# Up 4 as a seven-product block, a new order of the wide pieces, and earlier rounding of their operands

## The chip, the cores and the metric

The kernel runs on 1 core of a Trainium2 chip. The metric is device microseconds of one execution. Three timed runs of the kernel before took 2169.24 to 2171.04 us, median 2170.62 us. Engines are named as in the profile: PE (TensorE matmul), PEld (its weight load), DVE (VectorE), ACT (ScalarE), POOL (GpSimd), SP (the queue that issues the DMAs).

## The reference, cut to what matters

Two decoder layers on 256 tokens of width 2048 in float32, each a mixer (attention) and a gated feed-forward block (FFN), each with a residual and a LayerNorm. The change is in the two FFN blocks alone:

```
D_MODEL = 2048; SEQ = 256; DEPTH = 2
D_FF = -(-8 * D_MODEL // (3 * 256)) * 256          # 5632

def swiglu(x, w_gate, w_up, w_down):
    return (jax.nn.silu(x @ w_gate) * (x @ w_up)) @ w_down

    for layer in range(DEPTH):
        ...                                         # y = mixer(x)
        x = layer_norm(DEEPNORM_ALPHA * x + y, ln_g[layer, 0], ln_b[layer, 0])
        y = swiglu(x, ffn_w_gate[layer], ffn_w_up[layer], ffn_w_down[layer])
        x = layer_norm(DEEPNORM_ALPHA * x + y, ln_g[layer, 1], ln_b[layer, 1])
```

## The kernel before, in words

**Pieces.** Every weight matrix is cut into chunks of 512 output columns, and a chunk into pieces of 256 rows by 512 columns (512 KB, one DMA on SP). FFN chunks are Gate f, Up f (f = 0 to 10, eight pieces each) and Down chunks (five groups of four; four or six pieces each). A float32 product is made of three fp32r products, so each piece is split after it has landed: ACT rounds it (`wh`), DVE subtracts to get the residue (`wl`), and PE multiplies three times (`mm3`, L116 to L119). A plain piece is 12 matmuls of 512 columns.

**Wide pieces** (`c.S`; here "seven-product pieces") use a Strassen-Winograd scheme over two token blocks, two row blocks and two column halves: seven products instead of eight, each in three fp32r matmuls, 21 matmuls of 256 columns (`emit_s`). They cost more beside PE: three DVE subtractions in the landed piece (`sraw`, L380 to L383), a rounding of 1792 columns on ACT (`sh`, L386) and a residue of 1792 columns on DVE (`sl`, L389), and at the end of a chunk a drain of four PSUM banks sA, sB, sC, sD (`drain_s`, one copy on ACT, five adds on DVE) in place of the plain chunk's direct use of its bank. Before the change Gate 2 to Gate 10 and Up 8 are made so, 80 pieces in a layer.

**Order of the work.** `ffn_part` writes a list of visits (one visit is one piece on PE). The plain chunks stand in a fixed order; the wide pieces (`gates`) are strewn among them at a rate: after plain visit k, as many wide pieces have been placed as the sum `want` says. `near` sets a minimum at some ends of Up chunks.

**After an Up chunk** the product silu(Gate f) x Up f lies in `gt` (DVE, L1085 for a plain Up, in two halves; L1089 for a seven-product Up), and `h_T` transposes it on PE (tile `tp`, one call for each half of the tokens), evacuates it to YH on ACT (L113) and YL on DVE (L114). `after_up` says behind which two visits the two calls stand. While wide pieces run, plain chunks and transposes share four PSUM banks in two pairs: a new plain chunk takes the pair that the one before did not use, and transposes go to the pair that the current plain chunk does not use (`ptile`, `sw`, `PAIRS`).

**Splits.** After every visit `feed_more` issues the DMAs and splits that find a free buffer: four for plain pieces, two for wide ones while these run. For a wide piece `feed_split` issues the DVE subtractions at once, and owes (`owe`) the rounding and the residue; `pay` issues them within a later split, when the debt is at least one split old. DVE and ACT run their instructions in the order in which they are issued, so that order is what each of them waits in.

Of the kernel before, what the change touches and what calls it, by code (L numbers as in the profile page):

```python
# [53 lines left out]
def trunk_kernel(ctx: ExitStack, tc: tile.TileContext, x, ab_w_in, b_f, ab_w_out,  # L54
# [67 lines left out]
    visits = []  # L122
    chunks = {}

    def add_chunk(name, xs, kslots, srcs, tags=None):
        subs = []
        o = 0
        for n in srcs[0]:
            subs.append((n, o))
            o += n  # L130
        c = Chunk(name, xs, kslots, subs, srcs[1], tags or ("mm",) * len(subs))
        c.n = o
        chunks[name] = c
        return c

    def kmajor(c, hs=None):
        for h in (range(c.nh) if hs is None else hs):
            visits.append((c, h, (0, 1)))
# [18 lines left out]
    def lead_begin(c):  # L157
        for t in (0, 1):
            for h in range(LEAD):
                visits.append((c, h, (t,)))  # L160
        kmajor(c, range(LEAD, c.nh))

    def rows(w, k0, cols):
        return [(o, n, w[k0:k0 + 256, c0:c0 + n].rearrange("(k p) c -> p k c", p=P))
                for o, n, c0 in cols]
# [31 lines left out]

    GROUPS = ((0, 1), (2, 3), (4, 5), (6, 7), (8, 9, 10))
    NF = 11
    UPS = (8,)  # L200
    PLAIN = (0, 1)
    h_done = set()
    after_up = {}
    win = {}

    def ffn_part(layer):
        def wide(nm, w, f):
            return add_chunk(f"{nm}{layer}_{f}", "X", K16, ([512], lambda h: rows(
                w[layer], h * 256, [(0, 512, f * 512)])))

        def down(gi):
            grp = GROUPS[gi]
            slots = [4 * (f % 4) + k for f in grp for k in range(4)]
            for n in range(4):
                c = add_chunk(f"d{layer}_{gi}_{n}", "Y", slots, (
                    [512], lambda h, n=n: rows(
                        w_down[layer], grp[0] * 512 + h * 256, [(0, 512, n * 512)])))
                if gi == len(GROUPS) - 1 and n == 3:
                    (lead_final if layer == 1 else lead_end)(c)
                else:  # L220
                    kmajor(c)

        g0 = wide("g", w_gate, 0)
        g0.pair = 0
        lead_begin(g0)
        base = len(visits)
        for f in range(NF):
            if f == 1:
                kmajor(wide("g", w_gate, 1))
            c = wide("u", w_up, f)  # L230
            if f in UPS:
                c.S = True
            else:
                kmajor(c)
            if f in (1, 3, 5, 7):
                down(f // 2)
        down(len(GROUPS) - 1)
        flat = visits[base:]
        del visits[base:]
        ends = {}  # L240
        for f in range(NF):
            if f not in UPS:
                e = ends[f] = max(k for k, v in enumerate(flat) if v[0].name == f"u{layer}_{f}")
                o = e + 2 - f % 2
                after_up[layer, f] = [(v[0].name, v[1], v[2]) for v in flat[o:o + 3]]
        gates = []
        for f in range(len(PLAIN), NF):
            c = wide("g", w_gate, f)
            c.S = True
            gates += [(c, h, (0, 1)) for h in range(8)]  # L250
            if f in UPS:
                gates += [(chunks[f"u{layer}_{f}"], h, (0, 1)) for h in range(8)]
        near = {ends[f] + 2 for f in (1, 3, 5, 7, 9)}
        ns, want = 0, 0.0
        for k, v in enumerate(flat):
            visits.append(v)
            want = max(want + (0 if k < 9 else 0.53 if k < 118 else 0.7),
                       ns + 1 if k in near else 0)
            while ns < min(len(gates), int(want)):
                visits.append(gates[ns])  # L260
                ns += 1
                c = gates[ns - 1][0]
                f = int(c.name[3:])
                if ns % 8 == 0 and c.name[0] == "g" and f not in UPS:
                    assert k < ends[f] - 1, (k, ns, ends)
        assert ns == len(gates)
        for f in UPS:
            e = max(k for k, v in enumerate(visits) if v[0].name == f"u{layer}_{f}")
            after_up[layer, f] = [(v[0].name, v[1], v[2]) for v in visits[e + 1:e + 3]]

    w_out_part("oa", ab_w_out[0])
    ffn_part(0)
    wi = mla_w_in[0]
    c = add_chunk("m0", "X", K16, ([512], lambda h: rows(wi, h * 256, [(0, 512, 0)])))
# [8 lines left out]
    for nm in order:  # L283
# [8 lines left out]
        kmajor(c)  # L292
    w_out_part("om", mla_w_out[0])
    ffn_part(1)


# [49 lines left out]
    def feed_dma(j, halves=False):  # L346
        if j >= len(pieces):
            return False
        c, h = pieces[j]
        got = take(raw_free, j)  # L350
        if got is None:
            return False
        rslot_of[j] = got
        r = got[1]
        v = r[:, :2 * c.n].rearrange("p (k c) -> p k c", k=2)
        for o, n, src in c.src(h):
            for k in ((slice(0, 1), slice(1, 2)) if halves else (slice(0, 2),)):
                nc.sync.dma_start(v[:, k, o:o + n], src[:, k, :])
        raws[j] = r
        return True  # L360

    whole = {}
    owed = []

    def pay(step):

        for o in list(owed):
            while o["fns"] and (step == "all" or o["age"] >= 1 and step == o["fns"][0][0]):
                o["fns"].pop(0)[1]()
            if not o["fns"]:  # L370
                owed.remove(o)

    def owe(key, act, dve, age=0):
        owed.append({"key": key, "age": age, "fns": [("act", act), ("dve", dve)]})

    def split_s(j):
        r = raws.pop(j)
# [16 lines left out]
    def feed_split(j, halves=False, part=None):  # L394
        if j >= len(pieces):
            return False
        c, h = pieces[j]
        n = 2 * c.n
        if part != 1:
            got = take(w_free, j) if j in raws else None  # L400
            if got is None:
                return False
            slot_of[j] = got
            if c.S:
                new = split_s(j)
                for o in owed:
                    o["age"] += 1
                pay("act")
                pay("dve")
                owe(j, *new)  # L410
                return True
            r = raws.pop(j)
            wh, wl = got[1]
            wts[j] = (wh[:, :n].rearrange("p (k c) -> p k c", k=2),
                      wl[:, :n].rearrange("p (k c) -> p k c", k=2))
            whole[j] = (r, wh, wl)
        r, wh, wl = whole[j]
        cuts = [(0, c.n), (c.n, n)] if halves or part is not None else [(0, n)]
        if part is not None:
            cuts = [cuts[part]]  # L420
        for a, b in cuts:
            nc.scalar.activation(wh[:, a:b], r[:, a:b], AF.Copy)  # L422
            pay("act")
            nc.vector.tensor_tensor(wl[:, a:b], r[:, a:b], wh[:, a:b].bitcast(F32),  # L424
                                    op=ALU.subtract)
            pay("dve")
        if part != 0:
            whole.pop(j)
            raw_free.append(rslot_of.pop(j))
        for o in owed:  # L430
            o["age"] += 1
        return True
# [3 lines left out]
    def fetch():  # L436
        while fs["nd"] < len(pieces) and feed_dma(fs["nd"]):
            fs["nd"] += 1

    def feed_more(lim):  # L440
        fetch()
        while fs["nsp"] < min(lim, len(pieces)) and feed_split(fs["nsp"]):
            fs["nsp"] += 1
            fetch()

    def mm_s(o, xt, w, j, q, first, last):
        h, l = xt
        nc.tensor.matmul(o, h, w[0][:, q], start=first, stop=False)  # L448
        nc.tensor.matmul(o, h, w[1][:, q], start=False, stop=False)  # L449
        nc.tensor.matmul(o, l, w[0][:, q], start=False, stop=last)  # L450
# [375 lines left out]
                        load_T(hd - 8)  # L826
        return done

    cur = [0]
    for g in range(4):  # L830
        chunks[f"v{g}"].done = v_evac(g, chunks[f"v{g}"])
        for u in range(2):
# [520 lines left out]
    for i, (c, h, toks, *half) in enumerate(visits):  # L1353
# [21 lines left out]
        if last_use[c.name, h] == i:  # L1375
            j = pid[c.name, h]
            if c.name == "v0" and h in (0, 2, 4):
                x_T(h + 2)
                feed_more(h + 3)
                x_T(h + 3)  # L1380
            w_free.append(slot_of.pop(j))
            feed_more(min(i + 3 if i <= 4 else 8 + 17 * (i - 4) // 10, hold.get((c.name, h, toks), 10 ** 6)))
# [75 lines left out]
```

## Time and profile before

| | |
|---|---|
| timed runs, median of 3 | 2170.62 us (2169.24 to 2171.04) |
| profiled execution, its own time | 2170.17 us |
| its span, first to last instruction | 2168.3 us |
| PE busy | 2131.5 us, 98% of the span |
| DVE busy | 1639.8 us, 76% |
| ACT busy | 1046.3 us, 48% |
| mean granted TensorE clock | 0.994 |

The span is the time from the first to the last instruction; 1.9 us of the execution lie outside it. PE is busy nearly all the time, so time is lost or won where PE waits, where its clock is low, and in how many columns it multiplies. A busy share of PE is made of modelled ends; the step from one matmul's start to the next one's is the safer measure.

### The profile page before, as it was taken

The numbers are of one execution on the slowest core, as the hardware profiler recorded it, in microseconds if no ns is written. First come the engines' busy times: TensorE is split into PE (matmuls) and PEld (weight loads), VectorE is DVE, ScalarE is ACT, GpSimd is POOL, SyncE is SP. The second block draws the span as 40 slices with busy tenths as digits, with TensorE's granted clock in tenths as the row PEclk, the third lists the DMA queues.
The fourth block names the chain that finished last, engine by engine and source line by source line (L and its number), as shares of the span: only waits on it lengthen the run. The fifth ranks groups of instructions, "written<-read, shape, count | busy, mean of one in ns | idle before, by whom it ended". The sixth has DMA issues, their size and how long they took to land.

```text
span 2168.3 us, 31334 instructions
## 1 busy us (share of the span) xinstructions
PE 2131.5 (98%) x12426; PEld 1865.3 (86%) x12426; DVE 1639.8 (76%) x2117; ACT 1046.3 (48%) x1210; POOL 94.5 (4%) x142
## 2 busy tenths in 40 slices
PE   9999999999999999989999999999999999999998
PEld 9899998788888888878878998878888888887886
DVE  5555656788888888888866676598887888888875
ACT  5444544455444454444534665355544444454451
POOL 2100000100000000000001330010000000000000
PEclk9999999999999999999999999999999999999999
DMA  8565556555565555555765544745654555555582
GB/s 287 170 206 165 172 185 216 192 184 190 169 208 191 194 194 189 183 184 173 258 214 163 176 133 143 274 139 182 204 195 165 187 198 189 198 166 173 200 282 78
DMA packets 230338, 410.39 MB, mean 189 GB/s; under 512 B 14088, under 2 KB 58160, under 8 KB 229168
## 3 DMA queue, kind: packets, MB, share of 16 engines
q1 hardware_dynamic: 230192, 408.40, 56.5%
q8 instruction: 97, 1.59, 0.3%
q14 instruction: 49, 0.40, 0.1%
HBM read 402.56 MB, written 5.78 MB: 188 GB/s over the span
## 4 chain that ended last, share of the span: by engine, by line
PE 59%; issue 35%; DVE 3%; DMA 1%; POOL 1%; ACT 1%; SPq 0%; DVEq 0%; POOLq 0%; ACTq 0%
PE mm L117 12%; PE mm L118 12%; PE mm L119 12%; PE mm L507 3%; PE mm L509 3%; PE mm L511 3%; PE tp L597 2%; PE att L119 1%; PE att L118 1%; PE att L117 1%; PE sA L449 1%; PE sB L449 1%; PE sC L449 1%; PE sC L450 1%; PE sB L448 1%
## 5 line engine op out<-in xcount | busy, mean ns | idle before, releaser
L422 ACT ACTIVATE wh<-raw 128x1024 fp32r<-128x1024 f32 (+3 forms) x424 | 443.0, 1048 | 576.5 <-PE mm L119 358.2
L424 DVE TENSOR_TENSOR wl<-raw,wh 128x1024 fp32r<-128x1024 f32 (+3 forms) x424 | 511.5, 1211 | 193.0 <-ACT wh L422 186.4
L389 DVE TENSOR_TENSOR sl<-sraw,sh 128x1792 fp32r<-128x1792 f32 x160 | 323.5, 2022 | 37.6 <-ACT sh L386 37.4
L117 PE MATMUL mm<-wh,XH 128*128 128x512 f32 (+3 forms) x896 | 350.1, 391 | 0.0
L118 PE MATMUL mm<-wl,XH 128*128 128x512 f32 (+3 forms) x896 | 346.7, 387 | 0.0
L119 PE MATMUL mm<-wh,XL 128*128 128x512 f32 (+3 forms) x896 | 346.0, 386 | 0.0
L117 PE MATMUL mm<-wh,YH 128*128 128x512 f32 (+1 forms) x768 | 306.8, 400 | 11.3 <-DVE YL L114 10.7
L118 PE MATMUL mm<-wl,YH 128*128 128x512 f32 (+1 forms) x768 | 304.7, 397 | 0.0
L119 PE MATMUL mm<-wh,YL 128*128 128x512 f32 (+1 forms) x768 | 304.4, 396 | 0.0
L386 ACT ACTIVATE sh<-sraw 128x1792 fp32r<-128x1792 f32 x160 | 270.3, 1689 | 13.6 <-DVE sraw L383 10.6
L119 PEld LDWEIGHTS mm<-wh,XL 128*128 128x128 f32 x896 | 168.1, 188 | 36.6
L117 PEld LDWEIGHTS mm<-wh,XH 128*128 128x128 f32 x896 | 168.6, 188 | 31.2
L118 PEld LDWEIGHTS mm<-wl,XH 128*128 128x128 f32 x896 | 168.3, 188 | 30.6
L117 PEld LDWEIGHTS mm<-wh,YH 128*128 128x128 f32 x768 | 145.6, 190 | 43.4 <-DVE YL L114 11.4
L119 PEld LDWEIGHTS mm<-wh,YL 128*128 128x128 f32 x768 | 145.2, 189 | 35.2
L118 PEld LDWEIGHTS mm<-wl,YH 128*128 128x128 f32 x768 | 145.4, 189 | 30.7
L380 DVE TENSOR_TENSOR sraw<-sraw 128x512 f32<-128x512 f32 x160 | 109.5, 685 | 12.3 <-DMA sraw<-in_ffn_w_gate_dram 11.8
L507 PE MATMUL mm<-XH,wh 128*128 128x256 f32 x364 | 104.0, 286 | 0.0
L509 PE MATMUL mm<-XH,wl 128*128 128x256 f32 x364 | 102.3, 281 | 0.0
L511 PE MATMUL mm<-XL,wh 128*128 128x256 f32 x364 | 102.2, 281 | 0.0
L448 PE MATMUL sA<-sh,XH 128*128 128x256 f32 x320 | 92.1, 288 | 0.0
L449 PE MATMUL sA<-sl,XH 128*128 128x256 f32 x320 | 89.9, 281 | 1.8 <-DVE sl L389 1.8
(302 smaller groups left out, 4254.2 us busy)
## 6 DMA issues: line engine op xcount, KB each, us to landing
raw<-in_ffn_w_down_dram SPq DMA_DIRECT2D x160, 512.0 KB, 5.5
raw<-in_ffn_w_up_dram SPq DMA_DIRECT2D x155, 512.0 KB, 4.8
sraw<-in_ffn_w_gate_dram SPq DMA_DIRECT2D x149, 512.0 KB, 3.9
raw<-in_ab_w_in_dram SPq DMA_DIRECT2D x80, 256.0 KB, 3.1
raw<-in_ffn_w_gate_dram SPq DMA_DIRECT2D x27, 512.0 KB, 4.5
sraw<-in_ab_w_in_dram SPq DMA_DIRECT2D x48, 256.0 KB, 3.3
raw<-in_ab_w_out_dram SPq DMA_DIRECT2D x22, 512.0 KB, 3.5
sraw<-in_ffn_w_up_dram SPq DMA_DIRECT2D x21, 512.0 KB, 4.0
```

Of the source, the lines that this page charges most:

```text
L117: nc.tensor.matmul(o, lh, rh, start=start, stop=False)
L118: nc.tensor.matmul(o, lh, rl, start=False, stop=False)
L119: nc.tensor.matmul(o, ll, rh, start=False, stop=stop)
L386: nc.scalar.activation(sh, r[:, 256:2048], AF.Copy)
L389: nc.vector.tensor_tensor(sl, r[:, 256:2048], sh.bitcast(F32), op=ALU.subtract)
L422: nc.scalar.activation(wh[:, a:b], r[:, a:b], AF.Copy)
L424: nc.vector.tensor_tensor(wl[:, a:b], r[:, a:b], wh[:, a:b].bitcast(F32), op=ALU.subtract)
L448: nc.tensor.matmul(o, h, w[0][:, q], start=first, stop=False)
L449: nc.tensor.matmul(o, h, w[1][:, q], start=False, stop=False)
L507: nc.tensor.matmul(o, wh[:, kk, a:a + P], XH[:, slot, :], start=first, stop=False)
L509: nc.tensor.matmul(o, wl[:, kk, a:a + P], XH[:, slot, :], start=False, stop=False)
L511: nc.tensor.matmul(o, wh[:, kk, a:a + P], XL[:, slot, :], start=False, stop=last)
```

## The change

It does three things. Up 4 becomes a seven-product chunk too (`UPS = (4, 8)`), and joins the strewn list; the rates at which wide pieces are placed change. For seven-product Up chunks, the two `h_T` calls stand behind the first plain visit that begins a chunk after the Up's last piece, and behind the next plain one; before, they stood behind the two visits right after the Up. And `feed_more` issues everything owed as soon as the debt is one visit old.

```diff
-    UPS = (8,)
+    UPS = (4, 8)
...
-            want = max(want + (0 if k < 9 else 0.53 if k < 118 else 0.7),
+            want = max(want + (0 if k < 9 else 0.575 if k < 62 else 0.74 if k < 132 else 0.9),
                        ns + 1 if k in near else 0)
...
         for f in UPS:
             e = max(k for k, v in enumerate(visits) if v[0].name == f"u{layer}_{f}")
-            after_up[layer, f] = [(v[0].name, v[1], v[2]) for v in visits[e + 1:e + 3]]
+            rest = [v for v in visits[e + 1:] if not v[0].S]
+            o = next(k for k, v in enumerate(rest) if v[1] == 0)
+            after_up[layer, f] = [(v[0].name, v[1], v[2]) for v in rest[o:o + 2]]
...
+    cur = [0]
     whole = {}
     owed = []
...
     def owe(key, act, dve, age=0):
-        owed.append({"key": key, "age": age, "fns": [("act", act), ("dve", dve)]})
+        owed.append({"key": key, "age": age, "at": cur[0], "fns": [("act", act), ("dve", dve)]})
...
         while fs["nsp"] < min(lim, len(pieces)) and feed_split(fs["nsp"]):
             fs["nsp"] += 1
             fetch()
+        if any(cur[0] - o["at"] >= 1 for o in owed):
+            pay("all")
```

Both layers are changed alike. The attention parts are not touched. A layer's FFN keeps its number of visits; 88 of them, not 80, are seven-product pieces.

**Place 1: PE, layer 0, the first transpose of Up 8's result.** Before (`mm337` is a bank of a Down chunk that ends here, `mm339` and `mm340` are those of the next one, `tp338` the transposes, `gt220` the product):

```order
L117 MATMUL mm337_7982<-wh1_96,YH_70 128x512
L118 MATMUL mm337_7982<-wl1_97,YH_70 128x512
L119 MATMUL mm337_7982<-wh1_96,YL_71 128x512
L597 MATMUL tp338_8103<-ident_72,gt220_3529 128x128 x4
L117 MATMUL mm339_8116<-wh2_98,YH_70 128x512
L118 MATMUL mm339_8116<-wl2_99,YH_70 128x512
L119 MATMUL mm339_8116<-wh2_98,YL_71 128x512
L117 MATMUL mm340_8117<-wh2_98,YH_70 128x512
```

After, the transposes of the same result (`tp346`; `mm345` is a bank of a Down chunk at its first piece, `sA340` a seven-product piece of Gate 9):

```order
L117 MATMUL mm345_8244<-wh2_98,YH_70 128x512
L118 MATMUL mm345_8244<-wl2_99,YH_70 128x512
L119 MATMUL mm345_8244<-wh2_98,YL_71 128x512
L602 MATMUL tp346_8257<-ident_72,gt220_3529 128x128 x4
L453 MATMUL sA340_8207<-sh1_104,XH_68 128x256
L454 MATMUL sA340_8207<-sl1_105,XH_68 128x256
L455 MATMUL sA340_8207<-sh1_104,XL_69 128x256
```

Before, a new Down chunk starts right behind the transposes and takes the pair of banks in which they lie. Now the chunk has started before them, and they lie in the other pair, which the next chunk takes two plain and two seven-product pieces after the second transposes.

**Place 2: DVE, layer 0, the end of Up 3.** Before (the first five rows are the drain of Gate 4, L1085 the two halves of the product of Up 3):

```order
L479 TENSOR_TENSOR gt220_3529<-gt220_3529,sD273_5311 128x256
L480 TENSOR_TENSOR gt220_3529<-gt220_3529,sA272_5310 128x256
L481 TENSOR_TENSOR gt220_3529<-gt220_3529,sB274_5312 128x2x256
L483 TENSOR_TENSOR gt220_3529<-gt220_3529,sB274_5312 128x256
L484 TENSOR_TENSOR gt220_3529<-gt220_3529,sC275_5313 128x2x256
L380 TENSOR_TENSOR sraw0_92<-sraw0_92 128x512
L382 TENSOR_TENSOR sraw0_92<-sraw0_92 128x256
L383 TENSOR_TENSOR sraw0_92<-sraw0_92 128x256
L389 TENSOR_TENSOR sl0_103<-sraw1_93,sh0_102 128x1792
L424 TENSOR_TENSOR wl0_95<-raw3_91,wh0_94 128x1024
L1085 TENSOR_TENSOR gt221_3530<-gt221_3530,mm276_5513 128x512
L1085 TENSOR_TENSOR gt221_3530<-gt221_3530,mm277_5514 128x512
```

After, at the same product (now L1089; L392 is what was L389, L427 what was L424, L383 to L386 the subtractions):

```order
L392 TENSOR_TENSOR sl0_103<-sraw1_93,sh0_102 128x1792
L383 TENSOR_TENSOR sraw0_92<-sraw0_92 128x512
L385 TENSOR_TENSOR sraw0_92<-sraw0_92 128x256
L386 TENSOR_TENSOR sraw0_92<-sraw0_92 128x256
L427 TENSOR_TENSOR wl0_95<-raw3_91,wh0_94 128x1024
L392 TENSOR_TENSOR sl1_105<-sraw0_92,sh1_104 128x1792
L1089 TENSOR_TENSOR gt221_3530<-gt221_3530,mm276_5568 128x512
L1089 TENSOR_TENSOR gt221_3530<-gt221_3530,mm277_5569 128x512
L427 TENSOR_TENSOR wl1_97<-raw0_88,wh1_96 128x1024
```

Gate 4's drain no longer stands ahead of the product of Up 3; it now stands seven visits before it. In the new order it is Gate 2 whose drain is followed by one plain piece and the end of an Up (Up 1), but there the residue `sl` stands ahead of the drain and not behind it: after the drain come three subtractions and one `wl`, then the product.

**Place 3: DVE, layer 0, the end of Up 4.** Before, a plain chunk (L1085):

```order
L389 TENSOR_TENSOR sl1_105<-sraw0_92,sh1_104 128x1792
L380 TENSOR_TENSOR sraw1_93<-sraw1_93 128x512
L382 TENSOR_TENSOR sraw1_93<-sraw1_93 128x256
L383 TENSOR_TENSOR sraw1_93<-sraw1_93 128x256
L1085 TENSOR_TENSOR gt220_3529<-gt220_3529,mm298_6294 128x512
L1085 TENSOR_TENSOR gt220_3529<-gt220_3529,mm299_6295 128x512
L424 TENSOR_TENSOR wl1_97<-raw0_88,wh1_96 128x1024
L424 TENSOR_TENSOR wl2_99<-raw1_89,wh2_98 128x1024
```

After, a seven-product chunk (L932 is the residual add of a Down chunk, L484 to L489 the drain of Up 4 to `xt`, L1093 the product):

```order
L427 TENSOR_TENSOR wl0_95<-raw3_91,wh0_94 128x1024
L932 TENSOR_TENSOR X216_3525<-X216_3525,mm288_5982 128x512
L932 TENSOR_TENSOR X216_3525<-X216_3525,mm289_5983 128x512
L392 TENSOR_TENSOR sl0_103<-sraw1_93,sh0_102 128x1792
L484 TENSOR_TENSOR xt217_3526<-xt217_3526,sD281_5721 128x256
L485 TENSOR_TENSOR xt217_3526<-xt217_3526,sA280_5720 128x256
L486 TENSOR_TENSOR xt217_3526<-xt217_3526,sB282_5722 128x2x256
L488 TENSOR_TENSOR xt217_3526<-xt217_3526,sB282_5722 128x256
L489 TENSOR_TENSOR xt217_3526<-xt217_3526,sC283_5723 128x2x256
L1093 TENSOR_TENSOR gt220_3529<-gt220_3529,xt217_3526 128x1024
L383 TENSOR_TENSOR sraw0_92<-sraw0_92 128x512
```

The product now waits for a drain, and ahead of the drain stand the residual add of a Down chunk and one residue `sl` of 1792 columns. On PE the first transposes of this product stand behind one plain piece after the last piece of Up 4.

## Rows read from the trace of the kernel before

**Rows 1.** The page's busy times: engine, busy us (share), instructions

```profile
PE 2131.5 (98%) x12426; PEld 1865.3 (86%) x12426; DVE 1639.8 (76%) x2117; ACT 1046.3 (48%) x1210; POOL 94.5 (4%) x142
```

**Rows 2.** Timeline of PE, two plain pieces then a wide one: start, duration, instruction

```profile
701.75 0.39 PE L117 MATMUL mm<-wh,YH 128*128 128x512 f32 x1
...
707.36 0.28 PE L448 MATMUL sA<-sh,XH 128*128 128x256 f32 x1
...
709.83 0.39 PE L117 MATMUL mm<-wh,YH 128*128 128x512 f32 x1
```

**Rows 3.** Waits of PE: who waited, for whom, us in total, times, longest

```profile
PE sA L449 <- DVE sl L389: 1.8, 4, 0.8
```

**Rows 4.** Timeline of PE, layer 0, Up 8's first transposes; in brackets idle and releaser

```profile
963.00 0.66 PE L597 MATMUL tp<-ident,gt 128*128 128x128 f32 x4
969.38 0.80 PE L117 MATMUL mm<-wh,YH 128*128 128x512 f32 x1 [5.73 <-DVE YL L114]
...
974.12 0.39 PE L119 MATMUL mm<-wh,YL 128*128 128x512 f32 x1
```

**Rows 5.** Timeline of DVE behind those transposes

```profile
967.45 1.28 DVE L928 TENSOR_TENSOR X<-X,mm 128x512 f32<-128x512 f32 x2
968.64 0.68 DVE L114 TENSOR_TENSOR YL<-tp,YH 128x512 fp32r<-128x512 f32 x1
```

**Rows 6.** Timeline of PE, layer 1, the same place

```profile
1973.49 0.65 PE L597 MATMUL tp<-ident,gt 128*128 128x128 f32 x4
1973.90 0.48 PE L117 MATMUL mm<-wh,YH 128*128 128x512 f32 x1
...
1974.45 0.40 PE L119 MATMUL mm<-wh,YL 128*128 128x512 f32 x1
1979.87 0.80 PE L117 MATMUL mm<-wh,YH 128*128 128x512 f32 x1 [5.02 <-DVE YL L114]
```

**Rows 7.** Timeline of PE, layers 0 and 1, Up 3's first transposes

```profile
657.90 0.40 PE L119 MATMUL mm<-wh,YL 128*128 128x512 f32 x1
660.66 0.66 PE L597 MATMUL tp<-ident,gt 128*128 128x128 f32 x4 [2.36 <-DVE gt L1085]
...
1664.24 0.40 PE L119 MATMUL mm<-wh,YL 128*128 128x512 f32 x1
1667.60 1.12 PE L597 MATMUL tp<-ident,gt 128*128 128x128 f32 x4 [2.96 <-DVE gt L1085]
```

**Rows 8.** Stretches after three stalls: length, PE, PEld, DVE, ACT, POOL, clock, DMA, GB/s

```profile
967.20:973.90 6.70, 4.52 (x11) 3.59 (x12) 5.19 (x6) 0.00 (x0) 0.00 (x0) 0.50 0.52 164
...
1667.00:1673.60 6.60, 6.00 (x27) 5.91 (x28) 6.53 (x8) 1.66 (x2) 0.00 (x0) 0.50 0.90 296
1977.60:1984.20 6.60, 4.33 (x11) 3.35 (x12) 5.28 (x6) 0.00 (x0) 0.00 (x0) 0.50 0.53 165
```

**Rows 9.** Timeline of DVE, layer 0, Gate 4's drain to Up 3's product

```profile
651.41 0.42 DVE L479 TENSOR_TENSOR gt<-gt,sD 128x256 f32<-128x256 f32 x1 [1.54 <-ACT gt L478]
...
654.04 0.68 DVE L380 TENSOR_TENSOR sraw<-sraw 128x512 f32<-128x512 f32 x1
...
656.84 2.02 DVE L389 TENSOR_TENSOR sl<-sraw,sh 128x1792 fp32r<-128x1792 f32 x1 [1.20 <-ACT sh L386]
658.78 1.22 DVE L424 TENSOR_TENSOR wl<-raw,wh 128x1024 fp32r<-128x1024 f32 x1
659.92 1.28 DVE L1085 TENSOR_TENSOR gt<-gt,mm 128x512 f32<-128x512 f32 x2
```

**Rows 10.** Timeline of DVE, the work of a wide piece between two pieces

```profile
702.21 2.02 DVE L389 TENSOR_TENSOR sl<-sraw,sh 128x1792 fp32r<-128x1792 f32 x1 [0.37 <-ACT sh L386]
...
705.33 0.43 DVE L383 TENSOR_TENSOR sraw<-sraw 128x256 f32<-128x256 f32 x1
```

**Rows 11.** Groups of DVE, 975 to 1078 us: count, busy us, mean ns, idle before

```profile
L389 DVE TENSOR_TENSOR sl<-sraw,sh 128x1792 fp32r<-128x1792 f32 x14 | 28.3, 2019 | 0.7 <-ACT sh L386 0.7
```

**Rows 12.** The page's L389 group over the whole span, same columns

```profile
L389 DVE TENSOR_TENSOR sl<-sraw,sh 128x1792 fp32r<-128x1792 f32 x160 | 323.5, 2022 | 37.6 <-ACT sh L386 37.4
```

More of the change, by code (lines that the diff above doesn't have):

```diff
@@ L827, in qk_evac @@
         return done
-    cur = [0]
     for g in range(4):
```

## The prediction

> **What bounds the kernel now.** I read the busy times first: PE is busy 98% of the span, DVE 76%, ACT 48% [rows 1]. So the time is the sum of PE's steps and of the places where PE stands still, and DVE matters where PE waits for it. Then PE's timeline, for the step of a piece: two plain pieces take 707.36 - 701.75 = 5.61 us, 2.805 us each, and a wide piece 709.83 - 707.36 = 2.47 us [rows 2]. Then PE's waits and their places. In the FFN parts four places stand out, two in each layer, all behind `h_T`:
>
> - Up 8, layer 0: the transposes start at 963.00, and the next Down chunk's first matmul, due 0.41 us later (that step is 1973.49 to 1973.90), comes at 969.38 [rows 4, 6]. 969.38 - 963.41 = 5.97 us. It waits for YL, the evacuation of these very transposes, which DVE reaches at 968.64, after a residual add [rows 5]. In layer 1 the second bank's matmul is due at 1974.45 + 0.23 and comes at 1979.87: 5.19 us [rows 6].
> - Up 3: the transposes wait for the product of Up 3 (L1085). Due at 657.90 + 0.23, they come at 660.66: 2.53 us; in layer 1 due at 1664.24 + 0.24, they come at 1667.60: 3.12 us [rows 7].
>
> After three of the four the granted clock is 0.50, that is 1.2 GHz instead of 2.4, through the stretches of [rows 8]; after the stall of 2.53 us it stayed up. What such a stretch costs: 11 matmuls of 512 columns from 969.38 to 974.12 take 4.74 us [rows 4], at the full clock 11 x 0.234 = 2.57 us (a twelfth of 2.805). That is 2.17 us.
>
> **The change part by part.**
>
> *Products.* Eight pieces in each of two layers go from 2.805 to 2.47 us of PE: 16 x 0.335 = 5.4 us less, all of it on the path. The Trainium skill, "TensorE: Matmul & The Clock Gate", section "Back-to-back issue gap", speaks against this: it gives sustained steps of about 81 ns at 128 columns and about 131 ns at 512, so a matmul would cost much whatever its width. As an estimate from that page, 256 columns would take some 98 ns, 21 of them 2.05 us against 12 x 131 = 1.57 us, and the 16 pieces would cost 7.7 us more instead. The trace does not bear it out: 2.47 / 21 = 0.118 us at 256 columns and 0.234 us at 512 [rows 2], cost by column.
>
> *What the products add beside PE.* A wide piece takes DVE from 702.21 to the end of L383 at 705.76, 3.55 us [rows 10], a plain one 659.92 - 658.78 = 1.14 us [rows 9]. 16 x 2.41 us, and a drain of 654.04 - 651.41 = 2.63 us [rows 9] in each layer, make 44 us more on DVE over two FFN parts. ACT gets a longer rounding; it has half its time free [rows 1]. The cover is DVE's slack, and it is thinnest where wide pieces stand densest. From Up 8's first piece to Gate 10's last there are now 24 wide and 30 plain pieces (33 before). PE: 24 x 2.47 + 30 x 2.805 = 143.4 us. DVE: 24 x 3.55 + 30 x 1.14 = 119.4, three drains 7.9, four residual adds at 1.19 [rows 5] 4.8, three products at about 1.2 (the size of a residual add, or of a plain `wl`) 3.6, six YL at 0.68 4.1: 139.8 us. From Up 4 to Gate 8, 40 wide and 54 plain: PE 250.3 us; DVE 203.6 + five drains 13.2 + eight residual adds 9.5 + four products 4.8 + eight YL 5.4 = 236.5 us. So DVE fits, by 3.6 us and by 13.8 us, if it hardly waits. I take nothing for it but the 1.5 us below.
>
> *The place of `h_T` after a seven-product Up.* The pair of banks with Up 8's transposes is next taken two plain and two wide pieces later, 10.5 us, so YL has time. The stalls of 5.97 and 5.19 us and their low clock, 2.17 us each, go: 15.5 us. What is late next there is the residual add whose banks the transposes now take: it stands on DVE behind Up 8's drain and product, a split and a residue. A wait of some tenths there is part of the 1.5 us below.
>
> *The rates.* Gate 4's drain moves seven visits ahead of Up 3's product, so the stalls of 2.53 and 3.12 us and one low stretch of 2.17 us go: 7.8 us. In their place Gate 2's drain comes one plain piece before the end of Up 1. There the residue `sl` stands ahead of the drain. Before, the product began at 659.92, that is 7.4 us after the drain's chunk ended on PE (658.13 less two plain pieces = 652.52); without the `sl` of 1.94 us (658.78 - 656.84) and its wait of 1.20 us [rows 9] it begins about 4.3 us after, 4.8 if its `wl` waits for ACT. The transposes are due 5.6 us after and began 0.74 us after the product did (660.66 - 659.92). So no stall, with a few tenths to spare; if that cover is gone, up to 2.5 us in each layer.
>
> *Up 4.* Its product now waits for a drain, and PE transposes it one plain piece (2.805 us) later. Let T be the end of Up 4's last piece. The residual add ahead on DVE waits for the plain piece that ends at T - 2.47 us and takes 1.19 us, to T - 1.3; `sl` 1.94, to T + 0.6; drain 2.63, to T + 3.3; product about 1.15, to T + 4.4. A stall of 1.6 us; 1.2 if the first half of the residual add starts early, as its half of the piece ends early. I take 1.4 us, 2.8 us for both layers, and no low clock, since 2.53 us brought none. Bounds: 0, if the queue is ahead, to the 5.97 us and a low stretch of [rows 4], that is 16 us for two.
>
> *Earlier rounding and residue.* No instruction more; they stand one visit earlier on ACT and DVE. Queued behind the rounding are plain roundings on ACT, behind the residue plain residues; both are for pieces some visits away. The four waits of PE for `sl`, 1.8 us in all [rows 3], go. The two buffers of `sraw` come free earlier, so their DMAs are issued earlier on SP, in the same order between themselves. The sign could turn if DVE now stood in front of the ACT rounding; that is a rival.
>
> *The sum*, from the profiled execution's own 2170.17 us: - 5.4 - 15.5 - 7.8 - 1.8 + 2.8 + 1.5 (scattered waits of a DVE at over 95%, an estimate: about as much as the 1.8 us that PE waits for `sl` now) = - 26.2, that is 2144.0 us. The median of the runs lies 0.45 us above the profiled execution, so 2144.4. I say 2144 us.
>
> **The rivals.**
>
> *The stalls come back elsewhere.* Up 4 repeats the stall of the Up 8 type, or Up 1 that of Up 3. For it: drains, residual adds and transposes have not become fewer, DVE's slack in the dense stretch is 3.6 us, and one drain of 2.63 us eats most of it. Against: the transposes behind every drain, and the drain ahead of every product, have been counted above. If Up 1 stalls 2.5 us and Up 4 takes 6 + 2.2 us instead of 1.4, in both layers, 2 x (2.5 + 6.8) = 18.6 us come back: 2162.6. Cases of 2150 to 2167.
>
> *DVE becomes the bound (slower).* Issued together, the rounding (ACT) and the residue (DVE) leave nothing between them, and DVE stands at L389 until ACT has rounded. Now that wait is 37.4 us over 160 pieces, 0.23 us each [rows 12]; it is 0.37 us in the loose pattern [rows 10] and 1.20 us behind a drain [rows 9]. With a mean wait w the dense stretch is over PE's time by 24w - 3.6 us and the one before it by 40w - 13.8. At w = 0.6 that is 10.8 + 10.2 = 21 us a layer, 42 us in all: 2186 us. It decides from about w = 0.48, where 7.9 + 5.4 us a layer eat the whole gain. Against it: where wide pieces stand dense today, 975 to 1078 us, 14 of these residues waited 0.7 us together [rows 11], 0.05 us each, because a DVE that is late finds ACT done. The wait is there only when DVE has time for it.
>
> *Seven products save nothing on PE.* If 21 matmuls of 256 columns cost what 12 of 512 do, 0.134 us each, the 5.4 us are missing: 2149.4. The steps of [rows 2] speak against it: they are of exactly this code. The page named above would go further, to 7.7 us of loss; by that rule 2157.
>
> **How the numbers follow.** The forecast, 2138 to 2150, has 0.68: below, 26.2 + 2.8 + 1.5 us and a little more give 2139; above, Up 4's stall doubled and some 3 us more. Returned stalls (2150 to 2167) 0.20, DVE as the bound 0.08, no saving on PE 0.04. A range of 2138 to 2160 holds the first, the last and nearly half of the second, 0.81. About 0.2%, 4.3 us, is what a measurement of this kernel tells from no change. Faster by more than that: 0.68 + 0.04 + 0.15 = 0.87; within it the rest of the second case, 0.05; slower 0.08.
>
> **What would show it.** In the profile after: no idle of PE behind `h_T` of Up 8 and none before that of Up 3, in both layers; an idle of 1 to 2 us before Up 4's first transposes, for L1093; the granted clock at 1.00 through both FFN parts; PE's step of 2.47 us in Up 4; 176 residues of 1792 columns, and a mean wait for ACT ahead of them below 0.4 us; DVE near 1684 us busy. Wrong would be a stretch of low clock in a FFN part, or PE waiting for `sl` for more than some 5 us in all: then DVE is the bound there, and the time lies above 2150.

## The result and the profile after

The changed kernel takes 2146.49 us (median of 4 runs, 2146.04 to 2147.30), the kernel before 2169.93 us beside it (median of 4, 2169.09 to 2171.04). The ratio is 0.9892, with an interval of 0.9875 to 0.9909: 23.4 us faster. The forecast was 2144 us. The profiled execution took 2146.55 us with a span of 2144.7 us; all rows of after are from it. Profiles of different kernels also differ in how many stretches at the lower clock they have: before has three in its FFN parts, which the forecast priced at 2.17 us each, and after has none there and one in the attention between them.

The page of after has these busy times, and this group of the wide pieces' residues (count, busy us, mean ns, idle just before and its releaser):

```profile
PE 2120.4 (99%) x12570; PEld 1864.7 (87%) x12570; DVE 1674.0 (78%) x2173; ACT 1061.6 (50%) x1212; POOL 94.5 (4%) x142
...
L392 DVE TENSOR_TENSOR sl<-sraw,sh 128x1792 fp32r<-128x1792 f32 x176 | 356.2, 2024 | 64.6 <-ACT sh L389 63.9
```

Against [rows 1], PE is busy 11.1 us less with 144 matmuls more, DVE 34.2 us more. The mean wait for ACT ahead of a residue is 63.9 / 176 = 0.36 us, where [rows 12] had 0.23: it grew, and stayed below the 0.48 from which the forecast had DVE decide. PE's own waits (who, for whom, us in total, times, longest):

```profile
PE tp L602 <- DVE gt L1093: 2.7, 2, 1.4
PE tp L602 <- DVE gt L1089: 2.5, 3, 1.3
...
PE tp L602 <- DVE X L932: 1.0, 2, 0.8
PE sA L454 <- DVE sl L392: 0.4, 2, 0.2
```

The waits of [rows 4, 6] for YL are gone, those of [rows 7] at Up 3 too, and the waits for `sl` fell from 1.8 us [rows 3] to 0.4 us. What is left stands at three places. First Up 4, layer 0, on PE's timeline (start, duration, instruction, idle and releaser):

```profile
696.15 0.28 PE L453 MATMUL sA<-sh,XH 128*128 128x256 f32 x1
...
698.62 0.39 PE L117 MATMUL mm<-wh,YH 128*128 128x512 f32 x1
...
701.18 0.40 PE L119 MATMUL mm<-wh,YL 128*128 128x512 f32 x1
702.93 0.66 PE L602 MATMUL tp<-ident,gt 128*128 128x128 f32 x4 [1.35 <-DVE gt L1093]
```

The piece of Up 4 takes 698.62 - 696.15 = 2.47 us, as forecast. One plain piece later the transposes are due at 701.18 + 0.24 and come at 702.93: 1.51 us late, 1.51 us in layer 1 too (forecast 1.4). On DVE's timeline the queue ahead is the one that the forecast named: residual add, residue, drain, product.

```profile
695.65 1.38 DVE L932 TENSOR_TENSOR X<-X,mm 128x512 f32<-128x512 f32 x2
696.96 2.02 DVE L392 TENSOR_TENSOR sl<-sraw,sh 128x1792 fp32r<-128x1792 f32 x1
698.89 0.42 DVE L484 TENSOR_TENSOR xt<-xt,sD 128x256 f32<-128x256 f32 x1
...
701.65 1.22 DVE L1093 TENSOR_TENSOR gt<-gt,xt 128x1024 f32<-128x1024 f32 x1
```

Second, Up 1, where the forecast had no stall. PE, layers 0 and 1:

```profile
526.31 0.40 PE L119 MATMUL mm<-wh,YL 128*128 128x512 f32 x1
527.41 0.66 PE L602 MATMUL tp<-ident,gt 128*128 128x128 f32 x4 [0.70 <-DVE gt L1089]
...
1524.35 0.65 PE L602 MATMUL tp<-ident,gt 128*128 128x128 f32 x4 [1.30 <-DVE gt L1089]
```

They are 0.87 and 1.47 us late. This is DVE ahead of them (the last line is the product in layer 1), and the one rounding on ACT's timeline that matters:

```profile
513.34 2.02 DVE L392 TENSOR_TENSOR sl<-sraw,sh 128x1792 fp32r<-128x1792 f32 x1 [0.37 <-ACT sh L389]
515.28 0.68 DVE L383 TENSOR_TENSOR sraw<-sraw 128x512 f32<-128x512 f32 x1
...
518.80 2.02 DVE L392 TENSOR_TENSOR sl<-sraw,sh 128x1792 fp32r<-128x1792 f32 x1 [0.77 <-ACT sh L389]
520.75 0.41 DVE L484 TENSOR_TENSOR gt<-gt,sD 128x256 f32<-128x256 f32 x1
...
525.53 1.23 DVE L427 TENSOR_TENSOR wl<-raw,wh 128x1024 fp32r<-128x1024 f32 x1 [0.55 <-ACT wh L425]
526.68 1.28 DVE L1089 TENSOR_TENSOR gt<-gt,mm 128x512 f32<-128x512 f32 x2
...
1523.02 1.28 DVE L1089 TENSOR_TENSOR gt<-gt,mm 128x512 f32<-128x512 f32 x2
```

```profile
517.06 1.71 ACT L389 ACTIVATE sh<-sraw 128x1792 fp32r<-128x1792 f32 x1 [2.51 <-DVE sraw L386]
```

One residue (513.34) holds up the next piece's subtractions (from 515.28), so that ACT rounds it only at 517.06, so its residue runs from 518.80, and the drain behind it begins at 520.75. Before, the drain of Gate 4 had begun 1.11 us before its chunk ended on PE (651.41 against 652.52 [rows 9]); here it begins 0.22 us before (520.97 is the end). Those 0.9 us are what PE loses in layer 0. In layer 1 the product is as late, and the transposes begin 1.33 us behind its start (1523.02 to 1524.35) where layer 0 has 0.73; Up 3 before had the same difference, 1.33 us in layer 1 (1666.27 to 1667.60) against 0.74.

Third, Up 8: the YL stall is gone, and the transposes wait 0.39 us (due 964.91) and, in layer 1, 0.98 us for the residual add:

```profile
964.68 0.40 PE L119 MATMUL mm<-wh,YL 128*128 128x512 f32 x1
965.30 0.66 PE L602 MATMUL tp<-ident,gt 128*128 128x128 f32 x4 [0.22 <-DVE X L932]
```

Add 0.66 us at Up 0 of layer 1 and 0.94 us, start to start, of waits for `sl`, and PE loses 8.3 us in the FFN parts where the forecast had 2.8 + 1.5 = 4.3. The granted clock in the two dense stretches of layer 0, and in the one low stretch that after has behind its attention start (length, PE, PEld, DVE, ACT, POOL, clock, DMA, GB/s):

```profile
1203.20:1206.40 3.20, 3.20 (x17) 3.20 (x17) 0.96 (x1) 0.52 (x3) 2.95 (x6) 0.50 0.34 108
700.00:860.00 160.00, 158.65 (x950) 139.91 (x949) 145.28 (x171) 83.30 (x70) 0.00 (x0) 1.00 0.59 194
860.00:1046.00 186.00, 185.54 (x1110) 162.94 (x1109) 167.85 (x195) 95.63 (x81) 0.00 (x0) 1.00 0.59 197
```

No stretch of the FFN parts is at 0.50 as those of [rows 8] were. DVE is busy 91% and 90% of the dense stretches and PE hardly waits.

### The profile page after: what moved, and what is told of

Read it like the earlier page. It is cut to its first block, busy times and chain, and to the rows that moved or that the text cites. A ratio compares the mean times of both kernels' runs of the same rounds, so it can differ in the third digit from the quotient of the medians.

```text
span 2144.7 us, 31708 instructions
## 1 busy us (share of the span) xinstructions
PE 2120.4 (99%) x12570; PEld 1864.7 (87%) x12570; DVE 1674.0 (78%) x2173; ACT 1061.6 (50%) x1212; POOL 94.5 (4%) x142
## 4 chain that ended last, share of the span: by engine, by line
PE 58%; issue 35%; DVE 5%; ACT 1%; POOL 1%; DMA 0%; SPq 0%; DVEq 0%; ACTq 0%; POOLq 0%
PE mm L117 11%; PE mm L118 11%; PE mm L119 11%; PE mm L512 3%; PE mm L516 3%; PE mm L514 3%; PE tp L602 2%; PE att L118 1%; PE att L119 1%; PE att L117 1%; PE sA L454 1%; PE sB L454 1%; PE sC L454 1%; PE sC L455 1%; PE sB L453 1%
## 5 line engine op out<-in xcount | busy, mean ns | idle before, releaser
L425 ACT ACTIVATE wh<-raw 128x1024 fp32r<-128x1024 f32 (+3 forms) x403 | 417.5, 1040 | 416.2 <-PE mm L119 161.9
L427 DVE TENSOR_TENSOR wl<-raw,wh 128x1024 fp32r<-128x1024 f32 (+3 forms) x403 | 482.3, 1206 | 133.1 <-ACT wh L425 131.9
L392 DVE TENSOR_TENSOR sl<-sraw,sh 128x1792 fp32r<-128x1792 f32 x176 | 356.2, 2024 | 64.6 <-ACT sh L389 63.9
L389 ACT ACTIVATE sh<-sraw 128x1792 fp32r<-128x1792 f32 x176 | 298.9, 1698 | 145.1 <-DVE sraw L386 141.9
L117 PE MATMUL mm<-wh,XH 128*128 128x512 f32 (+3 forms) x820 | 319.9, 390 | 0.0
L118 PE MATMUL mm<-wl,XH 128*128 128x512 f32 (+3 forms) x820 | 316.8, 386 | 0.0
L119 PE MATMUL mm<-wh,XL 128*128 128x512 f32 (+3 forms) x820 | 316.3, 386 | 0.0
L119 PEld LDWEIGHTS mm<-wh,XL 128*128 128x128 f32 x820 | 153.9, 188 | 33.2
L117 PEld LDWEIGHTS mm<-wh,XH 128*128 128x128 f32 x820 | 154.4, 188 | 28.0
L118 PEld LDWEIGHTS mm<-wl,XH 128*128 128x128 f32 x820 | 154.1, 188 | 27.7
L383 DVE TENSOR_TENSOR sraw<-sraw 128x512 f32<-128x512 f32 x176 | 120.5, 685 | 0.0
```

What stands on the lines that cost most here:

```text
L117: nc.tensor.matmul(o, lh, rh, start=start, stop=False)
L118: nc.tensor.matmul(o, lh, rl, start=False, stop=False)
L119: nc.tensor.matmul(o, ll, rh, start=False, stop=stop)
L389: nc.scalar.activation(sh, r[:, 256:2048], AF.Copy)
L392: nc.vector.tensor_tensor(sl, r[:, 256:2048], sh.bitcast(F32), op=ALU.subtract)
```

## The experiments

Ratios are to the kernel before, run beside each set (2171.75 us beside e1, e2, e9 and e3; 2170.8 beside e5, e6 and e7; 2170.12 beside e11, e16 and e17). The times are medians; the rows are from one profiled execution of each kernel. The question behind the first three: the total came right, but is each term worth what the forecast gave it?

**e1: the place alone.** Before, with the new rule of `after_up` for Up 8.

```diff
-            after_up[layer, f] = [(v[0].name, v[1], v[2]) for v in visits[e + 1:e + 3]]
+            rest = [v for v in visits[e + 1:] if not v[0].S]
+            o = next(k for k, v in enumerate(rest) if v[1] == 0)
+            after_up[layer, f] = [(v[0].name, v[1], v[2]) for v in rest[o:o + 2]]
```

> The kernel before with one part of the change: the new place of the transposes behind a seven-product Up (Up 8 alone here). Theory: the two stalls behind Up 8's transposes (5.97 and 5.19 us) and the low clock after them go and nothing else changes: 15 us less, about 2155 us; the stalls before Up 3's transposes (2.5 and 3.1 us) and the one low stretch after the second stay. Rival (the stalls come back elsewhere): DVE is as late as before, so PE waits as long at the next transposes or bank: less than 8 us gained, above 2162 us.

2163.14 us, 0.9959 (0.9947 to 0.9972): 8.6 us, not 15, and nearer the rival's time than the theory's. PE's waits in it:

```profile
PE tp L599 <- DVE gt L1087: 5.8, 3, 3.0
PE tp L599 <- DVE X L930: 5.3, 2, 2.9
```

YL is gone from the list, and a new wait took half of its place: the transposes stand 2.50 and 3.10 us for the residual add whose banks they take. The waits of Up 3 (`gt`) are as in [rows 7]. The low clock behind Up 8 is gone, but its profile has a low stretch behind Up 3 in layer 0 and one in the attention that before has not (last section).

**e2: the earlier rounding and residue alone.** Before, with the change of `owe` and `feed_more`:

```diff
+        if any(cur[0] - o["at"] >= 1 for o in owed):
+            pay("all")
```

> The kernel before with one part of the change: rounding and residue issued one visit after the split. Theory as predicted: it only takes away PE's waits for sl, 1.8 us, so about 2168 us. Second reading, from the order of DVE (the residue now stands ahead of Gate 4's drain and not between the drain and Up 3's product): the stalls at Up 3 shrink to about 1 us each and lose their low clock (6 us), those at Up 8 shrink by about 2 us each: about 2158 us. Rival (DVE the bound): mean wait before the residue above 0.48 us and a time above 2170 us.

2158.77 us, 0.9939 (0.9927 to 0.9952): 13 us, as the second reading had it, where the forecast had priced this part at 1.8. PE's waits:

```profile
PE mm L117 <- DVE YL L114: 7.0, 2, 3.9
...
PE tp L600 <- DVE gt L1091: 1.7, 2, 0.8
PE tp L600 <- DVE gt L1087: 1.7, 2, 1.1
```

At Up 3 the stalls of 2.53 and 3.12 us are down to 0.70 and 1.30, with Gate 4's drain where it was; those for YL are 4.14 and 3.25 instead of 5.97 and 5.19, but ahead of them the transposes now come 1.0 us late in each layer, for Up 8's product (L1091).

**e9: both, with Up 4 plain and the old rates.** The edits of e1 and e2 together.

> The kernel before with the new place of the transposes and the earlier rounding, but Up 4 plain and the old rates. What is missing to the changed kernel is Up 4's seven products and the rates. Theory as predicted (rates took away Up 3's stalls, products give 5.4 us): 2170 - 15.4 - 1.8 = 2153 us. Second reading (the earlier residue already cures Up 3): 2170 - 15.4 - 6 - 1.8 = about 2147 us, so that Up 4's products and the rates are worth next to nothing on top, their 5.4 us being given back in stalls at Up 4, Up 1 and Up 8.

2148.96 us, 0.9897 (0.9882 to 0.9913). PE's waits, and DVE at the end of Up 3, layer 0:

```profile
PE tp L602 <- DVE X L932: 3.3, 2, 1.9
...
PE tp L602 <- DVE gt L1089: 1.7, 2, 1.1
```

```profile
650.09 2.02 DVE L392 TENSOR_TENSOR sl<-sraw,sh 128x1792 fp32r<-128x1792 f32 x1 [0.37 <-ACT sh L389]
652.03 0.41 DVE L484 TENSOR_TENSOR gt<-gt,sD 128x256 f32<-128x256 f32 x1
...
657.96 1.28 DVE L1089 TENSOR_TENSOR gt<-gt,mm 128x512 f32<-128x512 f32 x2
```

The drain begins at L484. Between it and the product there are now three subtractions and one `wl`; the residue that stood there in [rows 9], with its wait of 1.20 us, is ahead of the drain. So it is the earlier issue, not the new rates, that shortened Up 3's stall. With 8.6 and 13.0 us alone and 22.8 us together, these two edits are nearly all of the gain. Up 4 and the rates on top are worth 0.9897 - 0.9892, some 1 us by ratio, and 2.5 us by time, which the intervals don't tell from none. The two profiles say more. From the first transposes of X into an FFN part to those into the attention behind it, or to PE's last matmul, after takes 406.20 to 1134.23 and 1401.84 to 2134.11, e9 406.83 to 1137.29 and 1403.12 to 2136.30: 3.3 us less in the two FFN parts. In the attention between them after takes 1.8 us more; there it has its low stretch, and e9 has none.

**e3: after, without the earlier rounding and residue.** The two lines of e2 taken out of after.

> The changed kernel without the earlier rounding. Theory: the residue stands again between Gate 2's drain and Up 1's product, so Up 1 stalls 2.5 to 3.1 us in each layer (0.87 and 1.47 us with it), once or twice with low clock; Up 4's stall (1.51 us) shrinks since no residue stands ahead of its drain; waits for sl in the dense stretch grow by some us: about 2152 us. Rival: the early rounding is worth only the 1.8 us of sl waits: about 2148 us.

2209.79 us, 1.0176 (1.0159 to 1.0193): 63 us over after, 38 over the kernel before beside it. The expectation missed by far. PE's waits, then DVE's, then DVE's timeline at one of them, then a dense stretch:

```profile
PE sA L452 <- DVE sl L392: 41.1, 34, 3.3
```

```profile
DVE sraw L383 <- DMA sraw<-in_ffn_w_gate_dram: 85.9, 51, 4.1
...
DVE sraw L383 <- DMA sraw<-in_ffn_w_up_dram: 10.6, 10, 1.9
```

```profile
753.76 0.69 DVE L383 TENSOR_TENSOR sraw<-sraw 128x512 f32<-128x512 f32 x1 [2.50 <-DMA sraw<-in_ffn_w_gate_dram]
```

```profile
710.00:880.00 170.00, 158.03 (x917) 138.03 (x916) 140.94 (x165) 80.45 (x67) 0.00 (x0) 0.97 0.54 179
```

PE waits for the residue, and DVE waits 96.5 us for loads that it never waits for in after, while it is busy only 83%. SP issues the loads in the same order in both. The clock adds to it: the profile of e3 has nine stretches at 0.50 in its FFN parts, 34 us in all, where after has none; such a stretch costs at most half its length, so up to 17 us of this profiled execution, which took 2215.55 us. The theory: there are two landing buffers (`sraw`), and a buffer comes free with its residue; a residue issued one visit late frees it late, the load starts late, DVE, which runs in order, stands at that piece's subtraction, and so the next residue is late too. That SP's next load waits for the residue is in SP's own waits in e3, and the page of before already has a little of DVE's wait:

```profile
SPq L360 <- DVE sl L392: 1003.6, 169, 11.4
```

```profile
L380 DVE TENSOR_TENSOR sraw<-sraw 128x512 f32<-128x512 f32 x160 | 109.5, 685 | 12.3 <-DMA sraw<-in_ffn_w_gate_dram 11.8
```

The 11.8 us are 11.8 in e1 too and 0 in after, e2 and e9. So before the loop cost DVE little, and PE the 1.8 us of [rows 3]; with Up 4 and the new rates it costs much. Which of these two does it, no run tells apart. The rival: the residues are late by their place alone, and the loads only show it. The next two tell them apart.

**e16 and e17: half of each wide piece's load, without (e16) and with (e17) the earlier issue.** Only the first 128 of 256 rows are loaded; the other half of the numbers is left out, so the results mean nothing and only the time does.

```diff
-            for k in ((slice(0, 1), slice(1, 2)) if halves else (slice(0, 2),)):
+            for k in ((slice(0, 1), slice(1, 2)) if halves else (slice(0, 1),) if c.S else (slice(0, 2),)):
```

> The changed kernel without the earlier rounding (2209.8 us before), and of each wide piece only the first of its two 128-row halves is loaded, so 256 KB instead of 512; the second half keeps older numbers, all else is as it was. Theory (a loop: a late residue frees the landing buffer late, its DMA lands late, and so the next residue is late): with a shorter DMA most of the loop's excess goes, DVE's 96 us of waits for that DMA fall below 30 us, and the time to about 2165 us. Rival (the residue is late by its place in DVE's order alone): PE's 41 us of waits for sl stay, above 2195 us.

> Control: the changed kernel with the same half loads of the wide pieces. Theory (no DMA is on the path there, DVE waited 0 us for one): no change, 2144 to 2148 us. Rival (DMA bandwidth bounds something there): 2142 us or less.

e16 took 2175.3 us, 1.0027 (1.0018 to 1.0037), e17 2146.76, 0.9893 (0.9877 to 0.9910). A load lands in 2.8 us instead of 3.9. That alone takes 34.5 of e3's 63 us (32 by the ratios), and nothing from after. e16's waits on PE and on DVE:

```profile
PE sA L452 <- DVE sl L392: 17.8, 22, 2.1
```

```profile
DVE sraw L383 <- DMA sraw<-in_ffn_w_gate_dram: 33.4, 32, 2.9
```

The rival falls: with it e16 would have stayed near e3, above 2195 us. The theory's 2165 us and less than 30 us of DVE's waits were not reached either. That the load's time is on the path in e3 is shown. Three low stretches are left in e16's FFN parts, 10 us in all, so some of the 34.5 us is clock. Of the other 29 us a part still waits for loads (33.4 us on DVE); how much is place alone stays open.

**e5: the transposes one plain piece later**, in after, for Up 4 and Up 8.

```diff
-            after_up[layer, f] = [(v[0].name, v[1], v[2]) for v in rest[o:o + 2]]
+            after_up[layer, f] = [(v[0].name, v[1], v[2]) for v in rest[o + 1:o + 3]]
```

> The changed kernel with the transposes behind a seven-product Up one plain piece later still. Theory: Up 4's stalls (1.51 us twice) and Up 8's waits for the residual add (0.39 and 0.98 us) go, nothing else changes: 4.4 us less, about 2142 us. Rival: DVE is the bound there, and what is not waited for at the transposes is waited for at sl or at the next bank: less than 1.5 us gained.

2142.83 us, 0.9878 (0.9864 to 0.9891): 3.0 to 3.7 us below after (by ratio, by time). The theory's 2142 us came out. L1093 and L932 are gone from PE's waits; the waits for `sl` grew, 1.8 us instead of 0.4:

```profile
PE sA L454 <- DVE sl L392: 1.8, 4, 0.7
```

**e7: e5, and the first rate 0.56 instead of 0.575**, to move Gate 2's drain away from Up 1's product.

```diff
-            want = max(want + (0 if k < 9 else 0.575 if k < 62 else 0.74 if k < 132 else 0.9),
+            want = max(want + (0 if k < 9 else 0.56 if k < 62 else 0.74 if k < 132 else 0.9),
```

> As the one before, and the first rate 0.56 in place of 0.575, so that Gate 2's drain stands behind the end of Up 1 and not one plain piece ahead of it. Theory: Up 1's stalls (0.87 and 1.47 us) go too: 2.3 us less again, about 2140 us. Rival: shifted drains meet other transposes, no gain or a loss against the one before.

2141.81 us, 0.9872 (0.9858 to 0.9885), the lowest of all, below both kernels; against e5 1.0 us, which the runs (2140.97 to 2142.43, and 2141.78 to 2144.69) don't tell apart. The waits at Up 1 went, 2.3 us, and this one came:

```profile
PE mm L119 <- DVE YL L114: 2.0, 2, 1.0
```

**e11: e9 with the transposes one plain piece later** (Up 4 plain, old rates), the counterpart of e5.

> The kernel before with the earlier rounding and the transposes behind Up 8 two plain pieces after the start of the next chunk; Up 4 plain, old rates. Against the run with Up 4 as seven products and the same place of the transposes (2142.8 us) it says what Up 4 and the rates are worth without stalls at the transposes. Theory (the products are worth 5.4 us where the DVE queue gives nothing back): 2142.8 + 5.4 - 0.3 (stalls of Up 1 there against those of Up 3 here) - 1.9 (waits for sl there) = about 2146 us. Rival (products give back more than that in places not seen): 2144 us or less.

2145.78 us, 0.9890 (0.9875 to 0.9904). The theory's 2146 us came out. The transposes behind a seven-product Up wait in neither; e5 is some 3 us below, 2.6 by ratio and 2.4 in the FFN parts of the profiles, which is about what the expectation left of the products' 5.4 us (3.2). The intervals touch.

**e6: 0.46 us more DVE for each wide piece**, in after: one of the subtractions is issued twice.

```diff
         nc.vector.tensor_tensor(v[:, 6], v[:, 1], v[:, 5], op=ALU.subtract)
+        nc.vector.tensor_tensor(v[:, 6], v[:, 1], v[:, 5], op=ALU.subtract)
```

> The changed kernel with one of the three DVE subtractions of each wide piece issued twice: 0.46 us more of DVE for each of 176 pieces, 81 us in all, PE's work unchanged. Theory (DVE's room was priced right: 3.6 us in the dense stretch, 13.8 us in the one before): over by 24 x 0.46 - 3.6 = 7.4 and 40 x 0.46 - 13.8 = 4.6 us a layer, 24 us in all, about 2170 us, as waits of PE for sl. Rival (DVE has hidden slack, the dense stretch isn't near its limit): less than 6 us more. Rival (DVE already is the bound everywhere in the FFN parts): above 60 us more.

2175.05 us, 1.0025 (1.0014 to 1.0035): 28.6 us over after. PE's waits, and the dense stretches:

```profile
PE sA L455 <- DVE sl L393: 6.9, 10, 1.7
PE tp L603 <- DVE X L933: 6.2, 2, 3.4
PE tp L603 <- DVE gt L1090: 4.0, 4, 1.8
PE tp L603 <- DVE gt L1094: 3.5, 2, 1.8
PE mm L119 <- DVE YL L114: 2.2, 4, 1.0
```

```profile
702.00:866.00 164.00, 160.36 (x953) 140.34 (x951) 154.41 (x195) 83.83 (x70) 0.00 (x0) 1.00 0.56 189
866.00:1060.00 194.00, 186.69 (x1101) 162.88 (x1102) 178.36 (x223) 95.23 (x80) 0.00 (x0) 0.99 0.56 189
```

Of 176 x 0.46 = 81 us added to DVE, 28.6 reach the end; the slack that the forecast counted, a few us in the dense stretch and more elsewhere, is real and small. The time is near the theory's 2170 us, its mechanism only in part: by these rows 6.9 us are waits for `sl` (after: 0.4), and 15.9 us are waits around the transposes, for residual adds, products and YL (after: 6.2). What makes up the rest is not shown; three stretches at 0.50 in the FFN parts, 10 us in all, are part of it.

## Why the prediction was right, point by point

The time and the direction came out; the mechanisms that the forecast named are all in the trace. The shares that it gave them are not what the runs gave.

- **Products, 5.4 us.** The step of 2.47 us stands in Up 4 [rows 2]. The Trainium skill, "TensorE: Matmul & The Clock Gate", section "Back-to-back issue gap", would by the forecast's estimate from its figures have made this a loss of 7.7 us; the trace of after does not agree: 2.47 / 21 = 0.118 us for 256 columns. But 3.0 us of the 5.4 went back at once as Up 4's two stalls, and what Up 4 and the rates brought together over e9 is 1 to 2.5 us in the runs and 3.3 us in the FFN parts of the profiles.
- **Place of the transposes, 15.5 us.** The YL stalls went, as said. "A wait of some tenths" for the residual add was right only in the whole change (0.39 and 0.98 us): alone it is 2.50 and 3.10 us, and the place alone is worth 8.6 us (e1); with the earlier residue but the old rates PE still waits 3.3 us there (e9). So at Up 8 the new order helps, where the forecast credited it at Up 3.
- **Rates, 7.8 us.** This term is put down to the wrong edit. e2 and e9 keep the old rates and lose most of Up 3's stall. The order that the forecast read at Up 1 in the new kernel, residue ahead of the drain, is the work of the earlier issue, and in e2 it arises at Up 3 without any move of drains. The new rates then took away the remaining 0.70 and 1.30 us there and put 0.87 and 1.47 at Up 1.
- **Up 1, no stall.** This step failed: it let the drain begin when its chunk allowed, as in [rows 9], and did not ask whether the residue now ahead of it was over by then. The drain was 0.9 us late, which is the whole stall in layer 0. For layer 1 the forecast also took the 0.74 us of layer 0 from product to transposes; it is 1.33 us there, as it was before.
- **Up 4, 1.4 us.** 1.51 us in both layers; no low clock, as said.
- **Earlier rounding and residue, 1.8 us.** This is the mis-sized step. It counted the four waits for `sl` that PE showed, and not what the place in DVE's queue does to everything behind it. Measured: 13 us at the old density of wide pieces (e2), 14 us beside the new place (e1 to e9), 63 us at the new density (e3). The sentence in the forecast that the landing buffers "come free earlier, so their DMAs are issued earlier" names the loop that e3 shows, and was given no price.
- **DVE's room.** DVE was busy 1674.0 us (forecast 1684); the wait w came out at 0.36 us, below 0.48. The rival that DVE becomes the bound is near all the same: 0.46 us more for each wide piece (81 us of DVE) gave back all of the gain (e6).

The sum came right since what was over-priced (place, rates, 23.3 us) and what was under-priced (the earlier issue, 1.8 us) are together 25.1 us, and e9, with place and earlier issue, has 22.8: the forecast had read the new order as a whole, and divided it wrongly. That the wrong division did not spoil the time is luck: for the same change without the earlier issue its terms give 2146 us, and e3 took 2209.79. Of the 26.2 us that the forecast took off, the profiles show 25.4 us in the FFN parts (1485.7 us before, 1460.3 after), and the attention lost 1.8 us, with its low stretch at 1203 us. Within the FFN parts stalls cost 4.0 us more than forecast (8.3 against 4.3), so some 3 us of gains lie there that no run locates.

## What to carry to other kernels

When one engine's queue is in order, a deferred operation is priced by what stands behind it and by the buffer that it holds, not by the waits that the profile of before shows for its result. Here the sign stood on the page of before, as 11.8 us of DVE waiting for loads. Put the one that frees a landing buffer as early as its input allows, and only then raise the density. When several edits reorder the same queue, a right total says nothing about the shares; run each alone before dropping or repeating one. And when work is moved ahead of a drain, ask when the moved work itself can start.

## What the runs showed of the hardware

Whether a stall of PE is followed by the lower level of the clock (0.50 of 2.4 GHz) is not decided by the stall's length alone in these profiles. The wait for `krt` at the start of layer 1's attention is 1.7 to 1.8 us in all these kernels; in after it is

```profile
1201.65 0.36 PE L608 MATMUL tp<-identr,krt 128*128 128x128 f32 x2 [1.70 <-POOL krt L1203]
```

and the stretch at 0.50 from 1203.2 us follows it; the same wait was followed by such a stretch in e1, e3, e11 and e17 too, and by none in before, e2, e5, e6, e7, e9 and e16. Up 3's stall of 2.53 us left the clock up in before, and in e1, unchanged, it was followed by this one:

```profile
661.10:664.30 3.20, 3.20 (x16) 3.20 (x16) 3.20 (x3) 0.60 (x1) 0.00 (x0) 0.50 0.95 316
```

A stall of 3.10 us in e1 (Up 8, layer 1) was followed by none, one of 3.12 us in before by 6.6 us of it [rows 8]. The forecast took "no low clock, since 2.53 us brought none" for Up 4; that held, but the reason does not: such a stall was followed by the lower clock in one profile and not in another, and so few do not tell how likely it is.
